# Row sums that divide late: a DRAM detour for the softmax denominators of five head pairs

## The chip, the cores and the metric

One core of a Trainium2 chip runs the whole kernel. The metric is the device time of one execution in microseconds (us); the value of a kernel is the median of its runs. The engines are TensorE (PE, with its weight loads as PEld), VectorE (DVE), ScalarE (ACT), GpSimd (POOL) and SyncE (SP), which here only issues DMA transfers.

## The reference, cut to what matters

A trunk of two layers over 1024 tokens of width 1024 in fp32. Each layer is a token mixer of 12 heads (64 wide) beside a memory attention of 4 heads, then an output projection and a gated MLP with a causal convolution. Layer 0 mixes with causal softmax attention and a forget bias, layer 1 with rotary embedding and a dilated attention. What the change touches is the softmax and what follows it:

```python
sc = jnp.where(kpos[None, :] <= qpos[:, None], sc, NEG)
p = jax.nn.softmax(sc, axis=-1)
return jnp.einsum('bhqk,bhkd->bhqd', p.astype(v.dtype), v)
...
heads = jnp.concatenate([mix, mem_out], axis=1)
h = h + merge_heads(heads) @ w_out[layer]
```

Layer 1's three dilated branches, weighted by their log-sum-exps, come out as one softmax over all keys with a bias table, so both layers run the same block code.

## The kernel before

fp32 products are built from two fp32r halves ("hi" and "lo") with three matmuls per product. Activations lie feature-major: 128 partitions are two heads (a "head pair"), the free dimension is tokens.

A layer has an attention phase and an MLP phase. The attention phase first projects the memory and runs memory attention, then walks 96 blocks: 6 head pairs `p`, two heads `hh` each, 8 query blocks `i` of 128 tokens. For a block, `scores` (line 371) makes the scores on PE; one DVE instruction adds the bias, scales by -1/8 and keeps the row minimum (line 383); ACT takes the exponential into `y` and accumulates the row sum (line 387); DVE takes the reciprocal of the row sum (line 389) and multiplies `y` by it (line 390). Two blocks later `transpose_p` (line 392) transposes `y` on PE through one of two "tp" banks; ACT casts the bank to `pth` (line 397) and DVE subtracts to get `ptl` (line 398). Three blocks after the scores, and for two blocks at once, line 701 multiplies with the values on PE. `fold` (line 400) adds the halves of the result, ACT first (405) and DVE after it (406), and stores the tile in DRAM, `o_scr` (line 412); only for the last pair does it go straight to the output projection's operand.

Between the blocks a filler (`Fill`) puts the projections of the next pair on PE: `proj_q`, `proj_k` (with its moves of K halves between partitions on SP's queue, line 95), `proj_v`, and near the end `out_part`, the output projection over the first seven of eight result tiles. Its operand comes from `load_o` (line 246): it reads seven tiles back from `o_scr` in the order 0, 1, 2, 3, 6, 7, 4 into `oraw` (line 253; tag `sq`, five buffers of 128x512 that the rotary embedding and `fold` use too), ACT casts to the high half (line 254), GpSimd subtracts to the low half (line 255). Tiles 6 and 7 are the memory heads. It runs once per half of the tokens and layer. In layer 1 the rotary embedding of Q and K (lines 328 to 333) adds copies on ACT, a product on GpSimd and a sum on DVE.

PE's order is the program's (`manual_schedule`); the order on the other engines and on SP's queue comes from the framework's scheduler, and each engine then works through its list in order.

Of the kernel before, what the change touches and what calls it, by code (L numbers as in the profile page):

```python
# [6 lines left out]
F32 = mybir.dt.float32  # L7
R32 = mybir.dt.float32r
BF16 = mybir.dt.bfloat16
AF = mybir.ActivationFunctionType  # L10
ALU = mybir.AluOpType
AX = mybir.AxisListType

P = 128
T = 1024
KD = 8
NT = T // P
HT = 512
MT = 256
NMIX = 12  # L20
NPAIR = NMIX // 2
# [8 lines left out]
def trunk(ctx, tc, a, out):  # L30
    nc = tc.nc
    sb = ctx.enter_context(tc.tile_pool(name="sb", bufs=1))
    pp = ctx.enter_context(tc.tile_pool(name="ps", bufs=1, space=bass.MemoryType.PSUM))
    dram = ctx.enter_context(tc.tile_pool(name="dram", bufs=1, space=bass.MemoryType.DRAM))
# [11 lines left out]
    def yt(name):  # L46
        return sb.tile([P, T], F32, tag="P", name=name, bufs=3)

    def tab(name):
        return sb.tile([P, T], F32, tag="tab", name=name, bufs=3)  # L50

    def sqt(name, dt=F32):
        return sb.tile([P, HT], dt, tag="sq", name=name, bufs=5)

    def small(name, w=4, tag="m", bufs=8):
        return sb.tile([P, w], F32, tag=tag, name=name, bufs=bufs)
# [3 lines left out]
    def bank(tag, name="bk"):  # L60
        return pp.tile([P, HT], F32, tag=tag, name=name, bufs=NB[tag])
# [14 lines left out]
    trim = sb.tile([P, P], BF16, name="trim")  # L76
    gains = sb.tile([P, 7, KD], F32, name="gains")
    mhalf = sb.tile([P, 4], F32, name="mhalf")
    zero = sb.tile([P, MT], BF16, name="zero")
    nc.vector.memset(ones, 1.0)  # L80
    nc.vector.memset(mhalf, -0.5)
    nc.vector.memset(zero, 0.0)
    warm = small("warm")
    nc.scalar.activation(warm, mhalf, AF.Square)
    nc.scalar.dma_start(gains, a["gains"])
# [2 lines left out]
    nc.scalar.dma_start(trim, a["c_trim"])  # L88

    o_scr = [[dram.tile([P, T], F32, name=f"oscr{l}_{c}") for c in range(KD)] for l in range(2)]  # L90
    h_scr = [[dram.tile([P, HT], F32, name=f"hscr{c}_{h}") for h in range(2)] for c in range(KD)]
    c_scr = dram.tile([NMIX, T], F32, name="cscr")

# [19 lines left out]
    def x_tiles(half):  # L113
        return (sb.tile([P, KD, HT], R32, tag=f"xh{half}", name=f"xh{half}"),
                sb.tile([P, KD, HT], R32, tag=f"xl{half}", name=f"xl{half}"))
# [130 lines left out]
    def load_o(l, half):  # L246

        if (l, half) in O:
            return O[l, half]
        oh, ol = O[l, half] = x_tiles(half)  # L250
        for c in KORD[:-1]:
            raw = sqt("oraw")
            nc.sync.dma_start(raw, o_scr[l][c][:, half * HT:half * HT + HT])
            nc.scalar.copy(oh[:, c, :], raw)  # L254
            nc.gpsimd.tensor_tensor(ol[:, c, :], raw, oh[:, c, :].bitcast(F32), op=ALU.subtract)  # L255
        return oh, ol
# [21 lines left out]
    def attention_phase(l):  # L278
        with tc.manual_schedule(engines={mybir.EngineType.PE}):
# [88 lines left out]
                return proj_k(3 + 2 * p, half, ops[p], l == 1)  # L368


            def scores(y, m, qst, kst, klt, i, nk, bias, tri):
                qs = slice(i * P, (i + 1) * P)
                npc = (nk + HT - 1) // HT
                for pc in range(npc):
                    c0, c1 = pc * HT, min(nk, pc * HT + HT)
                    s = bank("s")
                    mask = tri and pc == npc - 1
                    sw = s[:, :c1 - c0]
                    nc.tensor.matmul(sw, lhsT=qst[:, qs], rhs=kst[:, c0:c1], start=True, stop=False)
                    nc.tensor.matmul(sw, lhsT=qst[:, qs], rhs=klt[:, c0:c1], start=False, stop=not mask)  # L380
                    if mask:
                        nc.tensor.matmul(s[:, c1 - c0 - P:c1 - c0], lhsT=identb, rhs=trim, start=False, stop=True)
                    nc.vector.tensor_tensor_reduce(  # L383
                        out=y[:, c0:c1], in0=sw, in1=bias(c0, c1), scale=-0.125,
                        scalar=BIG if pc == 0 else m[:, pc - 1:pc],
                        op0=ALU.add, op1=ALU.min, accum_out=m[:, pc:pc + 1])
                nc.scalar.activation(y[:, :nk], y[:, :nk], AF.Exp, bias=m[:, npc - 1:npc], scale=-1.0,  # L387
                                     accum_out=m[:, 2:3])
                nc.vector.reciprocal(m[:, 3:4], m[:, 2:3])
                nc.vector.tensor_scalar(y[:, :nk], y[:, :nk], m[:, 3:4], None, op0=ALU.mult)  # L390

            def transpose_p(y, j0, nj, ph, pl):
                tp = bank("tp").rearrange("p (j q) -> p j q", j=4)
# [6 lines left out]
            def fold(o, odd, c, half):  # L400

                rows = slice(64, 128) if odd else slice(0, 64)
                other = slice(0, 64) if odd else slice(64, 128)
                t = sqt("fold")
                nc.scalar.copy(t[rows, :], o[other, :])
                nc.vector.tensor_tensor(t[rows, :], o[rows, :], t[rows, :], op=ALU.add)
                if c == NPAIR - 1:
                    oh, ol = load_o(l, half)
                    nc.scalar.copy(oh[rows, c, :], t[rows, :])
                    nc.vector.tensor_tensor(ol[rows, c, :], t[rows, :], oh[rows, c, :].bitcast(F32), op=ALU.subtract)  # L410
                    return
                nc.sync.dma_start(o_scr[l][c][rows, half * HT:half * HT + HT], t[rows, :])

            def new_m():
                return small("m")
# [82 lines left out]
            def forget():  # L498

                cu = yt("cu")  # L500
                nc.scalar.dma_start(cu, a["c_cum"])
                w = NT * NMIX
                zf = z.rearrange("p t h -> p (t h)")
                e = [sqt(f"fz{i}")[:, :w] for i in range(4)]
                nc.vector.scalar_tensor_tensor(e[0], zf, -1.0, zf, op0=ALU.mult, op1=ALU.max)
                nc.scalar.activation(e[0], e[0], AF.Exp, scale=-1.0)
                nc.vector.tensor_scalar(e[1], e[0], 1.0, None, op0=ALU.add)
                nc.vector.tensor_scalar(e[2], e[1], -1.0, None, op0=ALU.add)
                nc.vector.tensor_tensor(e[0], e[0], e[2], op=ALU.subtract)
                nc.vector.reciprocal(e[2], e[1])  # L510
                nc.vector.tensor_tensor(e[0], e[0], e[2], op=ALU.mult)
                nc.scalar.activation(e[1], e[1], AF.Ln)
                nc.vector.tensor_tensor(e[0], e[0], e[1], op=ALU.add)
                lf = e[3]
                nc.vector.scalar_tensor_tensor(lf, zf, 0.0, e[0], op0=ALU.min, op1=ALU.subtract)
                yield None
                crow = yt("crow")
                for half in range(2):
                    ps = psp()
                    nt = 4 * half + 4  # L520
                    for t in range(nt):
                        c0 = max(t * P - half * HT, 0)
                        g0 = half * HT + c0 - t * P
                        nc.tensor.matmul(ps[:NMIX, c0:HT], lhsT=lf[:, t * NMIX:(t + 1) * NMIX],
                                         rhs=cu[:, g0:g0 + HT - c0], start=(t == 0), stop=(t == nt - 1))
                    nc.scalar.copy(crow[:NMIX, half * HT:half * HT + HT], ps[:NMIX, :])
                nc.sync.dma_start(c_scr, crow[:NMIX, :])
# [98 lines left out]
            if l == 0:  # L626
                f = forget()
# [32 lines left out]
            st = {}  # L660
            D = 2

            def emit_s(s):
                p, hh, i = seq[s]
                qst, kst, kl = ops[p]["q"], ops[p]["k"], ops[p]["kl"]
                if i == 0 and l == 0:
                    cb = tab("cb")
                    nc.sync.dma_start(cb, c_scr[2 * p + hh:2 * p + hh + 1, :].to_broadcast([P, T]))
                    st["cb"] = cb
                if l == 0:  # L670
                    cb = st["cb"]
                    bias = lambda c0, c1: cb[:, c0:c1]
                else:
                    bias = lambda c0, c1: toep[:, (7 - i) * P + c0:(7 - i) * P + c1]
                y, m = yt("y"), new_m()
                scores(y, m, qst[hh], kst[hh], kl[hh], i, (i + 1) * P, bias, l == 0)
                st["y", s] = y

            def emit_t(s):
# [29 lines left out]
            for s in range(len(seq) + D + 1):  # L709
                if s < len(seq):  # L710
                    p, i = s // 16, s % 16
# [246 lines left out]
```

## Time and profile before

| | |
|---|---|
| median of 3 runs | 2702.18 us (2698.43 to 2704.3) |
| profiled execution | 2700.07 us |
| its span, first to last instruction | 2698.3 us |
| mean granted TensorE clock | 0.983 |
| busy: PE, DVE, ACT, POOL | 2549.5, 1449.2, 1113.6, 889.8 us |

The attention phases lie at about 0 to 600 us and 1350 to 1950 us, the MLP phases after each. In the rows, "L390" is line 390; `out<-in` are the program's tile names; "<-" in brackets names what ended the idle time ahead of an instruction.

### The profile page before, as it was taken

To read this page: it belongs to the slowest core of one execution; us is meant where nothing else is said; L and a number is where in the kernel's file an instruction comes from. 1 tells how busy PE (TensorE), PEld (TensorE's weight loads), DVE (VectorE), ACT (ScalarE), POOL (GpSimd) and SP (SyncE) were. 2 spreads that over 40 slices of the span, in tenths; PEclk is the share of its full clock that TensorE was granted. 3 is DMA by queue.
4 is the path that set the end of the run, shared out by engine and by line. 5 is a ranking of instruction groups with operands and counts; after the bars stand their busy time and mean duration, and the time that the engine had idled before them with its cause. 6 is when DMAs were issued, how large, how long until landed. Compare 5 with 4: busy or idle time off the path is not lost. (4 is left out here: it accounts for less than half of the span.)

```text
span 2698.3 us, 34564 instructions
## 1 busy us (share of the span) xinstructions
PE 2549.5 (94%) x12808; PEld 2125.7 (79%) x12808; DVE 1449.2 (54%) x2879; ACT 1113.6 (41%) x2149; POOL 889.8 (33%) x650
## 2 busy tenths in 40 slices
PE   5899999989999999999998999989899999999997
PEld 4878888767888888888777787867688888888886
DVE  6667777565424343434766767665654343433345
ACT  5555555544313231223356767665433222222222
POOL 4210101454323232323552333335443232233232
PEclk8999999999999999999999999999999999999998
DMA  5121223422111111112431212133211111111112
GB/s 162 55 83 56 74 60 100 143 67 63 54 48 47 47 48 54 48 47 63 132 106 46 55 38 57 38 106 128 74 48 47 50 52 48 47 47 50 52 47 94
DMA packets 98896, 180.95 MB, mean 67 GB/s; under 512 B 12700, under 2 KB 15388, under 8 KB 98728
## 3 DMA queue, kind: packets, MB, share of 16 engines
q1 hardware_dynamic: 97864, 178.06, 21.6%
q8 instruction: 101, 1.65, 0.3%
q10 hardware_dynamic: 864, 0.69, 0.1%
q14 instruction: 67, 0.55, 0.1%
HBM read 148.24 MB, written 15.78 MB: 61 GB/s over the span
## 5 line engine op out<-in xcount | busy, mean ns | idle before, releaser
L110 POOL TENSOR_TENSOR wlo<-wraw,whi 128x512 fp32r<-128x512 f32 x450 | 590.2, 1331 | 1422.3 <-ACT whi L109 1328.3
L162 PE MATMUL bk<-xh,whi 128*128 128x512 f32 x2112 | 857.4, 406 | 34.6 <-ACT xh L254 11.6
L163 PE MATMUL bk<-xl,whi 128*128 128x512 f32 x2112 | 832.4, 394 | 5.8 <-POOL xl L255 3.1
L164 PE MATMUL bk<-xh,wlo 128*128 128x512 f32 x2112 | 831.5, 394 | 1.0 <-POOL wlo L110 1.0
L109 ACT CAST whi<-wraw 128x512 fp32r<-128x512 f32 x450 | 268.6, 616 | 644.9 <-PE bk L163 442.4
L162 PEld LDWEIGHTS bk<-xh,whi 128*128 128x128 f32 x2112 | 402.5, 191 | 116.9 <-ACT xh L254 13.6
L164 PEld LDWEIGHTS bk<-xh,wlo 128*128 128x128 f32 x2112 | 400.7, 190 | 86.8 <-POOL wlo L110 1.7
L163 PEld LDWEIGHTS bk<-xl,whi 128*128 128x128 f32 x2112 | 402.2, 190 | 83.2 <-POOL xl L255 6.4
L162 PE MATMUL bk<-gh,whi 128*128 128x512 f32 x704 | 276.1, 392 | 1.2 <-DVE h L259 1.1
L776 DVE SCALAR_TENSOR_TENSOR gate<-bk,cw,gate 128x511 f32<-128x511 f32 (+1 forms) x176 | 131.3, 746 | 271.5 <-ACT gate L774 270.0
L163 PE MATMUL bk<-gl,whi 128*128 128x512 f32 x704 | 274.6, 390 | 0.0
L164 PE MATMUL bk<-gh,wlo 128*128 128x512 f32 x704 | 274.5, 390 | 0.0
L259 DVE TENSOR_TENSOR h<-h,bk 128x512 f32<-128x512 f32 x208 | 141.7, 685 | 236.3 <-PE bk L164 236.3
L387 ACT ACTIVATE y<-y,m 128x128 f32<-128x128 f32 (+1 forms) x192 | 149.2, 778 | 106.5 <-DVE m L383 104.1
L776 DVE SCALAR_TENSOR_TENSOR val<-bk,cw,val 128x511 f32<-128x511 f32 (+1 forms) x176 | 131.1, 745 | 114.6 <-ACT val L774 113.0
L398 DVE TENSOR_TENSOR ptl<-bk,pth 128x512 fp32r<-128x512 f32 (+3 forms) x288 | 152.8, 551 | 66.1 <-ACT pth L397 65.4
L397 ACT CAST pth<-bk 128x512 fp32r<-128x512 f32 (+3 forms) x288 | 131.0, 479 | 93.1 <-PE bk L396 90.8
L396 PE MATMUL bk<-ident,y 128*128 128x128 f32 x864 | 130.2, 277 | 33.1 <-DVE ptl L398 32.9
L162 PEld LDWEIGHTS bk<-gh,whi 128*128 128x128 f32 x704 | 132.6, 188 | 31.2 <-DVE h L259 2.8
L163 PEld LDWEIGHTS bk<-gl,whi 128*128 128x128 f32 x704 | 132.6, 188 | 27.7 <-issue 0.5
L164 PEld LDWEIGHTS bk<-gh,wlo 128*128 128x128 f32 x704 | 132.4, 188 | 27.6
L792 DVE TENSOR_TENSOR gl<-val,gh 128x1024 fp32r<-128x1024 f32 x44 | 53.9, 1226 | 175.4 <-ACT gh L791 175.4
(160 smaller groups left out, 3585.6 us busy)
## 6 DMA issues: line engine op xcount, KB each, us to landing
wraw<-in_wu SPq DMA_DIRECT2D x176, 256.0 KB, 2.8
wraw<-in_wd SPq DMA_DIRECT2D x104, 256.0 KB, 2.8
wraw<-in_wo SPq DMA_DIRECT2D x64, 256.0 KB, 2.8
wraw<-in_wq SPq DMA_DIRECT2D x56, 256.0 KB, 2.9
oscr<-fold SPq DMA_DIRECT2D x56, 128.0 KB, 2.2
oraw<-oscr SPq DMA_DIRECT2D x28, 256.0 KB, 3.7
cb<-cscr SPq DMA_DIRECT2D x12, 512.0 KB, 3.9
wraw<-in_wv SPq DMA_DIRECT2D x20, 256.0 KB, 2.9
```

The source lines that it names most:

```text
L109: nc.scalar.copy(hi[:, w], raw[:, :n])
L110: nc.gpsimd.tensor_tensor(lo[:, w], raw[:, :n], hi[:, w].bitcast(F32), op=ALU.subtract)
L162: nc.tensor.matmul(ps, lhsT=whi(k), rhs=xhi(k), start=(first and k == 0), stop=False)
L163: nc.tensor.matmul(ps, lhsT=whi(k), rhs=xlo(k), start=False, stop=False)
L164: nc.tensor.matmul(ps, lhsT=wlo(k), rhs=xhi(k), start=False, stop=(last and k == nk - 1))
L259: nc.vector.tensor_tensor(H[half](n), (src or H[half])(n), ps, op=ALU.add)
L387: nc.scalar.activation(y[:, :nk], y[:, :nk], AF.Exp, bias=m[:, npc - 1:npc], scale=-1.0, accum_out=m[:, 2:3])
L396: nc.tensor.transpose(tp[:, jj, :], y[:, j * P:(j + 1) * P], ident)
L397: nc.scalar.copy(ph, tp[:, :nj, :])
L398: nc.vector.tensor_tensor(pl, tp[:, :nj, :], ph.bitcast(F32), op=ALU.subtract)
L776: nc.vector.scalar_tensor_tensor(t[:, o + d:o + HT], ps[:, :HT - d], w(2 - d), t[:, o + d:o + HT], op0=ALU.mult, op1=ALU.add)
L792: nc.vector.tensor_tensor(gl, v, gh.bitcast(F32), op=ALU.subtract)
```

## The change

For the first five head pairs the exponentials stay undivided. The row sums of four blocks gather in one tile of four columns, `den`; after each fourth block DVE takes the reciprocal of all four columns, and a DMA writes them into a row of DRAM, `r_scr`, one row of 1024 tokens per head. The stored result tiles are thus too large by the row sum. When `load_o` reads back a tile of these pairs, it also reads the two reciprocal rows, each broadcast to 64 partitions, and DVE multiplies the tile by them before the cast. The last pair and the memory heads keep dividing their probabilities. An unused tile of zeros and its memset go.

```diff
-    zero = sb.tile([P, MT], BF16, name="zero")
-    nc.vector.memset(zero, 0.0)
...
+    r_scr = [[dram.tile([2, T], F32, name=f"rscr{l}_{c}") for c in range(NPAIR - 1)] for l in range(2)]
...
             raw = sqt("oraw")
-            nc.sync.dma_start(raw, o_scr[l][c][:, half * HT:half * HT + HT])
+            hs = slice(half * HT, half * HT + HT)
+            nc.sync.dma_start(raw, o_scr[l][c][:, hs])
+            if c < NPAIR:
+                rb = sqt("orb")
+                for hh in range(2):
+                    nc.sync.dma_start(rb[64 * hh:64 * hh + 64, :], r_scr[l][c][hh:hh + 1, hs].to_broadcast([64, HT]))
+                nc.vector.tensor_tensor(raw, raw, rb, op=ALU.mult)
             nc.scalar.copy(oh[:, c, :], raw)
...
                 nc.scalar.activation(y[:, :nk], y[:, :nk], AF.Exp, bias=m[:, npc - 1:npc], scale=-1.0,
-                                     accum_out=m[:, 2:3])
-                nc.vector.reciprocal(m[:, 3:4], m[:, 2:3])
-                nc.vector.tensor_scalar(y[:, :nk], y[:, :nk], m[:, 3:4], None, op0=ALU.mult)
+                                     accum_out=m[:, 2:3] if den is None else den)
+                if den is None:
+                    nc.vector.reciprocal(m[:, 3:4], m[:, 2:3])
+                    nc.vector.tensor_scalar(y[:, :nk], y[:, :nk], m[:, 3:4], None, op0=ALU.mult)
...
-                scores(y, m, qst[hh], kst[hh], kl[hh], i, (i + 1) * P, bias, l == 0)
+                if p < NPAIR - 1 and i % 4 == 0:
+                    st["den"] = small("den", 4, "den", 3)
+                den = st["den"] if p < NPAIR - 1 else None
+                scores(y, m, qst[hh], kst[hh], kl[hh], i, (i + 1) * P, bias, l == 0,
+                       None if den is None else den[:, i % 4:i % 4 + 1])
+                if den is not None and i % 4 == 3:
+                    nc.vector.reciprocal(den, den)
+                    with nc.allow_non_contiguous_dma(reason="one value per query"):
+                        nc.sync.dma_start(r_scr[l][p][hh, (i - 3) * P:(i + 1) * P].rearrange("(t q) -> q t", q=P), den)
```

## Rows read from the trace of the kernel before

**Rows 1.** Busy by stretch: us, PE, PEld, DVE, ACT, POOL, PEclk, DMA share, GB/s.

```profile
600.00:1400.00 800.00, 791.17 (x3524) 653.21 (x3523) 359.74 (x546) 245.64 (x383) 292.74 (x206) 1.00 0.21 64
...
165.00:455.00 290.00, 278.86 (x1801) 241.67 (x1800) 210.34 (x566) 162.12 (x372) 35.83 (x28) 0.99 0.25 71
1510.00:1800.00 290.00, 265.45 (x1663) 232.07 (x1663) 198.99 (x534) 194.14 (x418) 99.30 (x77) 0.99 0.18 49
```

**Rows 2.** Waits of PE, 165 to 455 us: total us, times, longest.

```profile
PE bk L396 <- DVE ptl L398: 8.8, 10, 1.8
...
PE bk L701 <- DVE ptl L398: 0.8, 2, 0.5
```

**Rows 3.** Waits of PE, 1510 to 1800 us.

```profile
PE bk L396 <- DVE ptl L398: 17.7, 14, 2.7
PE bk L701 <- DVE ptl L398: 5.2, 10, 1.0
...
PE bk L380 <- DMA kla<-kla: 0.3, 1, 0.3
```

**Rows 4.** Groups by line: busy us, mean ns, idle before them and its releaser.

```profile
L390 DVE TENSOR_SCALAR y<-y,m 128x128 f32<-128x128 f32 (+1 forms) x192 | 115.0, 599 | 5.0
...
L389 DVE RECIPROCAL m<-m 128x1 f32<-128x1 f32 x192 | 31.1, 162 | 88.6 <-ACT y L387 87.9
```

**Rows 5.** Timelines of DVE and ACT near 450 us: start, us, instruction.

```profile
448.50 1.01 DVE L390 TENSOR_SCALAR y<-y,m 128x128 f32<-128x128 f32 x1
...
450.27 1.16 DVE L398 TENSOR_TENSOR ptl<-bk,pth 128x512 fp32r<-128x512 f32 x2
...
449.11 0.97 ACT L397 CAST pth<-bk 128x512 fp32r<-128x512 f32 x2
```

**Rows 6.** Timelines of DVE and ACT near 1599 us.

```profile
1599.79 0.89 DVE L398 TENSOR_TENSOR ptl<-bk,pth 128x512 fp32r<-128x512 f32 x2
...
1598.74 0.75 ACT L397 CAST pth<-bk 128x512 fp32r<-128x512 f32 x2
```

**Rows 7.** Timeline of DVE near 1509 us, layer 1.

```profile
1508.48 0.69 DVE L331 TENSOR_TENSOR ropeq<-bk,ropec 128x512 f32<-128x512 f32 x1 [1.29 <-ACT ropeqs L330]
...
1509.83 1.74 DVE L333 TENSOR_TENSOR ropeq<-ropeq,ropeqs 128x512 f32<-128x512 f32 x1
```

**Rows 8.** Timeline of PE near 1510 us, layer 1.

```profile
1509.84 0.66 PE L396 MATMUL bk<-ident,y 128*128 128x128 f32 x4 [1.12 <-DVE ptl L398]
1512.09 0.65 PE L396 MATMUL bk<-ident,y 128*128 128x128 f32 x4 [1.60 <-DVE ptl L398]
```

**Rows 9.** Busy by stretch, around the wait near 450 us.

```profile
445.00:455.00 10.00, 8.18 (x48) 7.00 (x47) 8.44 (x22) 6.18 (x15) 2.59 (x2) 0.84 0.34 107
```

**Rows 10.** Waits of PE over the whole span, for the cast in `load_o`.

```profile
PE bk L162 <- ACT xh L254: 11.6, 3, 5.2
```

**Rows 11.** Timelines of PE at the two first halves of `load_o`.

```profile
485.76 0.67 PE L162 MATMUL bk<-xh,whi 128*128 128x512 f32 x1 [3.88 <-ACT xh L254]
...
1819.48 0.79 PE L162 MATMUL bk<-xh,whi 128*128 128x512 f32 x1 [5.22 <-ACT xh L254]
...
1824.83 0.79 PE L162 MATMUL bk<-xh,whi 128*128 128x512 f32 x1 [2.53 <-ACT xh L254]
```

**Rows 12.** Timeline of POOL, first half of `load_o`, layer 1.

```profile
1824.86 7.46 POOL L255 TENSOR_TENSOR xl<-oraw,xh 128x512 fp32r<-128x512 f32 x6 [3.83 <-ACT xh L254]
```

**Rows 13.** Busy by stretch, first half of `load_o`, layer 0.

```profile
484.00:494.00 10.00, 7.00 (x18) 4.15 (x18) 1.37 (x5) 4.85 (x10) 6.69 (x6) 0.66 0.87 252
```

**Rows 14.** Group of line 437, DVE.

```profile
L437 DVE TENSOR_TENSOR ym<-ym,mm 128x512 f32<-128x512 f32 x32 | 22.7, 709 | 0.9
```

**Rows 15.** DMA issues: count, KB each, median us to landing.

```profile
oscr<-fold SPq DMA_DIRECT2D x56, 128.0 KB, 2.2
oraw<-oscr SPq DMA_DIRECT2D x28, 256.0 KB, 3.7
...
gains<-in_gains ACTq DMA_DIRECT2D x1, 28.0 KB, 3.8
```

More of the change, by code (lines that the diff above doesn't have):

```diff
@@ L368, in pair_k, with scores @@
                 return proj_k(3 + 2 * p, half, ops[p], l == 1)
-            def scores(y, m, qst, kst, klt, i, nk, bias, tri):
+            def scores(y, m, qst, kst, klt, i, nk, bias, tri, den):
                 qs = slice(i * P, (i + 1) * P)
```

## The prediction

> **What bounds the kernel now.** I read busy time by stage first, then who TensorE (PE) waited for, then the timelines of the places where it waited. In the MLP between 600 and 1400 us PE is busy 791 of 800 us and VectorE (DVE) 360 [rows 1], so nothing that the change does to DVE can count there. The attention phases are where PE has holes. In pairs 0 to 4 of layer 0 (165 to 455 us) it is idle 290.00 - 278.86 = 11.1 us, in those of layer 1 (1510 to 1800 us) 290.00 - 265.45 = 24.6 us [rows 1]. DVE is only 69 to 73% busy there, so it is no bound by its sum; it hurts where it is late. PE's order is written out by hand and the change does not touch it; what counts is only how long PE stands before a given matmul.
>
> PE waits in those stretches almost only for `ptl` (line 398), DVE's subtraction, which frees the PSUM bank that the next transposes want, or makes the low half that the value matmuls read: 8.8 + 0.8 = 9.6 us in layer 0 [rows 2], 17.7 + 5.2 = 22.9 us in layer 1 [rows 3]. That is the whole pool from which a relief of DVE can be paid, 32.5 us. The reader is to see how small it is beside the work removed.
>
> **What goes.** 160 of 192 blocks lose the reciprocal (line 389) and the scaling (line 390). DVE's busy time falls by 160/192 of 31.1 + 115.0 us, 122 us, and the 87.9 us in which it stood before line 389 until ScalarE's (ACT) exponential was through goes in the same share, 73 us [rows 4]. Added on DVE: 40 reciprocals of 4 columns at line 389's 0.16 us (6 us; each still waits for its exponential, but once in four blocks) and 20 products of 128x512. DVE is relieved by some 100 us of work.
>
> How much of it reaches PE is read from what stands ahead of `ptl`. Three kinds of place:
> - DVE itself is the line. Around 450 us a scaling of 1.01 us stands in front, and `ptl` starts at 450.27; ACT's casts for it began at 449.11 and two took 0.97, so the first was done near 449.7 [rows 5]. Without the scaling `ptl` starts some 0.57 us sooner, and then ACT's cast is what is late. PE's wait there is the longest of layer 0, 1.8 us [rows 2]: a third of it goes.
> - The fold. `ptl` starts at 1599.79, with scaling and reciprocal ahead of it on DVE; ACT's two casts ran from 1598.74 for 0.75 [rows 6], the first ready near 1599.33, so 0.46 us goes.
> - Rotary embedding, layer 1 alone. DVE stood 1.29 us until ACT's copies `ropeqs` were through, and its sum `ropeq` then took 1.74 us [rows 7]. Nothing of this is removed. PE waited 1.12 and 1.60 us there [rows 8]; the pair of waits comes three times, and a wait of 2.7 us [rows 3] twice, the same `ropeq` behind it: 13.5 of the 22.9 us. I take nothing off them.
>
> So of 9.6 us and of 22.9 - 13.5 = 9.4 us I take 45%: 8.5 us. DVE's shorter queue also lets the row minima, and so the exponentials that wait for them, start sooner; no row prices that. It is 0 if ACT is late in any case, and at most the rest, 24 us; I take 4, near zero, because in all three kinds ACT comes last. Then the granted clock: the 10 us around the wait near 450 have 0.84 instead of 1.00 [rows 9], 1.6 us of PE work; with that wait cut I take 1.5 back. Relief: 8.5 + 4 + 1.5 = 14 us, bounds 4 and 32.
>
> **What comes.** `load_o` reads back result tiles, four times in all (two halves, two layers). Each time five of seven tiles now take three transfers instead of one, a slot of the `sq` pool (5 buffers) for the row sums, and a product on DVE ahead of ACT's cast. PE waits three times for these casts, 11.6 us in all [rows 10], and the timeline has all three in first halves: 3.88 (layer 0), 5.22 and 2.53 (layer 1) [rows 11]. Second halves are not waited for; their loads lie ahead of the matmuls, and I cost them at 0, with 3 us each if that cover is gone. In the first halves PE stands with nothing else to do, so a longer load goes straight into the span.
>
> Its price per first half, from both sides. Below: 0, if the three transfers overlap and GpSimd's subtraction, 7.46 us for six tiles anyway [rows 12], stays the pace. By bytes: ten transfers of 128 KB more are 1.31 MB; in the heart of the load the queues are 0.87 busy and move 252 GB/s [rows 13], so 5.2 us. By slots: a round of load (3.7 us [rows 15]), product (0.7), cast (0.5, as in [rows 5]) and subtraction (1.24) is 6.1 us, and five slots hold two and a half tiles with their sums, so five such tiles take 12.3 us where subtraction needs 6.2: 6.1 us more. I take 3.5 us, between nothing and the bytes, for the first tile is loaded ahead of the rest and the two unscaled tiles catch up; and 0.5 us because PE runs this stretch at a granted clock of 0.66 [rows 13], between its two levels of 1.2 and 2.4 GHz, and stays there longer. Twice 4 is 8 us; bounds 0 and 14.
>
> The product is taken at 0.71 us from line 437, the same shape from SBUF [rows 14]; from above it is line 333's 1.74 us, two SBUF inputs while GpSimd worked [rows 7]. The Trainium skill, "SBUF — State Buffer", Who interferes with whom, says that a DVE instruction with two SBUF inputs contends with GpSimd's reads of SBUF. The row of 1.74 us agrees; by the rule every product in `load_o` stands beside GpSimd's subtractions, and the slot bound grows by about 1 us a round.
>
> The 40 writes of row sums (128 partitions x 4 values) go out on SyncE's (SP) queue between the K moves (line 95), the stores of `fold` and the weights. A write waits for its reciprocal, and what stands behind it waits too: mostly weight loads, far ahead of PE. Its own duration no row shows: from below 2.2 us (a 128 KB store), from above four times the 3.8 us of a transfer with 128 short rows, since it has 512 pieces, 15 us [rows 15]. I take 4 us, near the store, and at that nothing is late. Memset and `zero` tile: nothing, they lie in the start, ahead of the first loads' landing.
>
> **Sum.** -14 + 8 = -6 us. The profiled execution took 2700.07 us; 2700.07 - 6 = 2694, and as it lies 2.1 us below the median of the runs, 2696 is the forecast. 0.2% is 5.4 us, about what a measurement of this kernel can tell from no change.
>
> **Rivals.**
> - *The load becomes the longer wait (slower).* If slots set the pace, each first half costs 6.1 us and, for products held up by GpSimd, 1 us in each of two rounds; second halves lose their cover, 3 us each: 2 x (8.1 + 3) = 22 us against 14: +8, 2710. For it: the queues are nearly full there already, and PE stands idle. Against it: first halves alone were waited for. It decides from a load stretch that is 7 us longer than before in each layer.
> - *The small writes hold up the K moves (slower).* In layer 1 PE already waited 0.3 us for a K move to land [rows 3], so these have no slack. At the bound of 15 us instead of 4 a move right behind a write is 11 us late; at five pairs of layer 1 that is 55 us, and at a third of it, since not every move follows a write closely, 18: -6 + 18 = +12, 2714. The Trainium skill, "DMA: Bandwidth & Descriptors", Rules for kernel authors, says that a transfer with a strided last dimension becomes one descriptor per element; no row of before shows such a transfer.
> - *DVE's relief pays in full (faster).* If the exponentials move up with the minima, most of the 32.5 us goes, less rope waits that ACT and GpSimd make: 24 us, with the load at 6: -18, 2684.
> - *No change to be seen.* If ACT is late everywhere, 4 us of relief meet 4 of load: 2702.
>
> **Chances.** The forecast 0.48 (half of it beyond 0.2%, half within), relief in full 0.20, load 0.16, K moves 0.08, no change 0.08. Faster by over 0.2%: 0.24 + 0.20 = 0.44. Within: 0.24 + 0.08 = 0.32. Slower: 0.24. The range reaches to the rivals on both sides, 2681 to 2714; the forecast's own range is 2688 to 2703.
>
> **What would show it.** DVE's busy time near 1350 us; PE's waits for `ptl` down from 32.5 to about 20 us with the rope ones standing; first-half waits for the cast of `load_o` longer, some 7 us more over both layers; no wait for a K move. Wrong would be: `ptl` waits gone altogether, or as large as before; PE waiting in the second halves of `load_o`; a write of row sums that lands in over 8 us.

## The result: slower, 2724.35 us

The changed kernel took 2724.35 us, the median of four runs (2723.70 to 2725.90), beside 2701.43 for the kernel before, measured with it: a ratio of 1.0085, 95% interval 1.007 to 1.010. It is slower by 23 us, above the top of the predicted range. The profiled execution took 2725.9 us, 2724.1 of it span. VectorE's (DVE's) busy time fell from 1449.2 to 1374.3 us, so the work did go; the time did not follow.

Busy by stretch, changed kernel (us, PE, PEld, DVE, ACT, POOL, granted clock, DMA share, GB/s). The first and third rows answer to [rows 1].

```profile
165.00:455.00 290.00, 285.18 (x1861) 248.83 (x1860) 168.17 (x450) 166.62 (x384) 35.64 (x28) 1.00 0.32 72
455.00:600.00 145.00, 119.37 (x574) 93.43 (x574) 84.99 (x177) 65.09 (x132) 54.39 (x41) 0.88 0.41 121
1510.00:1800.00 290.00, 265.74 (x1668) 232.35 (x1669) 160.65 (x413) 194.05 (x421) 100.78 (x77) 0.99 0.22 51
1800.00:1950.00 150.00, 117.86 (x562) 92.86 (x562) 85.77 (x180) 70.55 (x143) 62.59 (x47) 0.87 0.39 116
```

The same view of the kernel before, for the two stretches that were not shown:

```profile
455.00:600.00 145.00, 128.27 (x662) 102.79 (x662) 90.06 (x202) 75.59 (x153) 60.11 (x46) 0.95 0.34 105
1800.00:1950.00 150.00, 129.19 (x637) 103.98 (x636) 85.80 (x179) 75.12 (x149) 76.42 (x58) 0.94 0.36 114
```

In the pairs of layer 0 DVE sheds 42 us and TensorE (PE) gains 6.3 of its 11.1 idle us. In the pairs of layer 1 DVE sheds 38 us and PE gains 0.3. In the two stretches where results are read back, PE is busy 9 and 11 us less than before, at a lower granted clock. These stretches are fixed in time, and work that comes later falls out of them; the comparison matmul by matmul, below, is the safer one.

PE's waits over the whole span (total us, times, longest):

```profile
PE bk L402 <- DVE ptl L404: 28.0, 22, 2.7
PE bk L161 <- ACT xh L259: 26.5, 6, 12.6
PE bk L161 <- ACT xh L415: 12.5, 2, 6.5
...
PE bk L384 <- DMA ka<-ka: 0.6, 2, 0.4
...
PE bk L385 <- DMA kla<-kla: 0.3, 1, 0.3
```

Line 259 is the cast of `load_o`: 11.6 us in three waits [rows 10] have become 26.5 in six. Line 415 is the cast of pair 5's own fold, which ends a second half. For K moves PE waits 0.9 us in all, where it was 0.3 [rows 3].

PE's timeline at the places of [rows 11], then at the two second halves:

```profile
481.72 0.79 PE L161 MATMUL bk<-xh,whi 128*128 128x512 f32 x1 [8.60 <-ACT xh L259]
...
498.82 0.50 PE L161 MATMUL bk<-xh,whi 128*128 128x512 f32 x1 [1.59 <-ACT xh L259]
...
1833.51 0.80 PE L161 MATMUL bk<-xh,whi 128*128 128x512 f32 x1 [12.64 <-ACT xh L259]
...
564.24 0.79 PE L161 MATMUL bk<-xh,whi 128*128 128x512 f32 x1 [6.00 <-ACT xh L415]
...
1915.49 0.80 PE L161 MATMUL bk<-xh,whi 128*128 128x512 f32 x1 [6.50 <-ACT xh L415]
```

PE's order is the same in both kernels (12808 matmuls), so the start of the n-th in one trace can be set beside that of the n-th in the other; the times below are those of the kernel before. At 455 us the changed kernel is 9.0 us ahead. The first half of layer 0 turns that into 5.3 us behind at 540 us (14.3 us lost), its second half into 7.6 at 600 us (2.3 more). The pairs of layer 1 win back 1.1 by 1800 us. Its first half costs 14.3 by 1880 us, its second 4.7 by 1950; the end is 25.8 us behind. In sum some 10 us gained, 28.6 lost in first halves, 7.0 in second halves. One and the same kernel traced twice (e10 and e18 below) differs from itself by up to 3.4 us in this way, so the first halves stand clear of that, and a second half by itself hardly.

The two first halves, matmul for matmul: layer 0, then layer 1, first the kernel before,

```profile
455.00:540.00 85.00, 78.14 (x429) 63.73 (x429) 51.16 (x133) 46.45 (x100) 30.27 (x23) 0.96 0.43 132
...
1800.00:1880.00 80.00, 68.22 (x353) 55.97 (x352) 44.71 (x109) 45.22 (x95) 40.42 (x32) 0.91 0.48 148
```

then the changed one:

```profile
446.00:545.30 99.30, 83.69 (x430) 66.66 (x429) 55.33 (x131) 44.27 (x96) 28.41 (x22) 0.88 0.45 127
...
1806.50:1900.90 94.40, 73.48 (x353) 58.68 (x352) 51.12 (x113) 42.95 (x91) 38.73 (x30) 0.84 0.47 137
```

PE stands 8.8 us longer in the one and 9.1 in the other. The rest, 5.6 and 5.3 us, is the same matmuls taking longer, at a granted clock of 0.88 and 0.84 where it was 0.96 and 0.91.

The two waits at second halves were shorter in the kernel before:

```profile
556.59 0.49 PE L162 MATMUL bk<-xh,whi 128*128 128x512 f32 x1 [3.69 <-ACT xh L409]
...
1890.48 0.49 PE L162 MATMUL bk<-xh,whi 128*128 128x512 f32 x1 [2.56 <-ACT xh L409]
```

What is late there now is on DVE's timeline of the changed kernel:

```profile
558.41 0.69 DVE L258 TENSOR_TENSOR oraw<-oraw,orb 128x512 f32<-128x512 f32 x1 [2.38 <-POOL wlo L109]
559.02 0.68 DVE L388 CUSTOM_DVE_ANT_0 y<-bk,cb 128x512 f32<-128x512 f32 x1
...
1909.67 0.69 DVE L258 TENSOR_TENSOR oraw<-oraw,orb 128x512 f32<-128x512 f32 x1 [2.89 <-DMA orb<-rscr]
1910.28 0.68 DVE L388 CUSTOM_DVE_ANT_0 y<-bk,toep 128x512 f32<-128x512 f32 x1
```

PE has made the last block's scores by 555.2 and 1905.8 us, but their row minimum (line 388) stands in DVE's order behind the product of the last tile read back, and DVE is idle 2.38 and 2.89 us until that tile's row is there. It lands at 558.29 and 1909.55 us. GpSimd's `wlo`, which the first line names, ended in the same instant, but the product reads nothing of it. The exponential, the fold and the fold's cast all follow the minimum.

How a first half goes now is seen on SyncE's (SP's) queue in layer 0, where PE arrives at 473 us:

```profile
472.81 0.58 SPq L253 DMA_DIRECT2D oraw<-oscr  x1
473.48 0.46 SPq L94 DMA_DIRECT2D kb<-kb  x1
474.64 0.46 SPq L418 DMA_DIRECT2D oscr<-fold  x1
475.16 0.59 SPq L94 DMA_DIRECT2D klb<-klb  x1
476.00 1.11 SPq L257 DMA_DIRECT2D orb<-rscr  x2
```

and on DVE:

```profile
480.33 0.69 DVE L258 TENSOR_TENSOR oraw<-oraw,orb 128x512 f32<-128x512 f32 x1 [3.22 <-DMA orb<-rscr]
482.15 1.42 DVE L258 TENSOR_TENSOR oraw<-oraw,orb 128x512 f32<-128x512 f32 x1 [1.13 <-DMA orb<-rscr]
...
496.81 0.69 DVE L388 CUSTOM_DVE_ANT_0 y<-bk,cb 128x512 f32<-128x512 f32 x1 [6.13 <-PE bk L385]
...
497.42 0.69 DVE L258 TENSOR_TENSOR oraw<-oraw,orb 128x512 f32<-128x512 f32 x1
```

The raw tile is asked for at 472.81, its row only at 476.00, behind two K moves and a fold's store. Product, cast and PE follow at 480.33, 481.05 and 481.72. The last tile shows a second thing: its product is queued on DVE behind a row minimum that itself waits for PE's scores, and PE then stands 1.59 us for the cast behind that product.

DMA issues of the changed kernel (count, KB each, median us to landing), which answer to [rows 15], and one wait on SP's queue:

```profile
oscr<-fold SPq DMA_DIRECT2D x56, 128.0 KB, 2.2
...
orb<-rscr SPq DMA_DIRECT2D x40, 128.0 KB, 4.0
...
rscr<-den SPq DMA_DIRECT2D x40, 2.0 KB, 8.4
```

```profile
SPq L253 <- POOL xl L260: 16.2, 12, 2.3
```

The loads of raw tiles waited 16.2 us, twelve times, for GpSimd (POOL) to give back a slot of the `sq` pool; in the kernel before it was 10.3 us, seven times.

### The profile page after: what moved, and what is told of

Same layout as the page of the kernel before. It is cut to its first block, busy times and chain, and to the rows that moved or that the text cites. A ratio compares the mean times of both kernels' runs of the same rounds, so it can differ in the third digit from the quotient of the medians.

```text
span 2724.1 us, 34573 instructions
## 1 busy us (share of the span) xinstructions
PE 2558.5 (94%) x12808; PEld 2132.2 (78%) x12808; DVE 1374.3 (50%) x2618; ACT 1111.9 (41%) x2149; POOL 892.5 (33%) x650
## 5 line engine op out<-in xcount | busy, mean ns | idle before, releaser
L161 PE MATMUL bk<-xh,whi 128*128 128x512 f32 x2112 | 859.1, 407 | 55.8 <-ACT xh L259 26.5
```

The source lines that it names most:

```text
L161: nc.tensor.matmul(ps, lhsT=whi(k), rhs=xhi(k), start=(first and k == 0), stop=False)
```

## Experiments

Each median stands beside that of the kernel before measured with it; line numbers in the rows are each kernel's own.

| run | us | before | ratio, 95% interval |
|---|---|---|---|
| e1_relief | 2688.54 | 2701.74 | 0.9951, 0.9937 to 0.9966 |
| e2_load | 2741.66 | 2701.74 | 1.0152, 1.0137 to 1.0167 |
| e3_nowrite | 2732.90 | 2701.74 | 1.0115, 1.0098 to 1.0131 |
| e4_slots | 2710.95 | 2701.74 | 1.0037, 1.0023 to 1.0050 |
| e5_const | 2701.68 | 2700.04 | 1.0007, 0.9997 to 1.0016 |
| e6_first | 2708.69 | 2700.04 | 1.0032, 1.0020 to 1.0044 |
| e7_fold | 2724.72 | 2700.04 | 1.0092, 1.0075 to 1.0109 |
| e8_folddve | 2717.21 | 2700.04 | 1.0062, 1.0047 to 1.0077 |
| e9_early | 2709.49 | 2699.90 | 1.0038, 1.0023 to 1.0053 |
| e10_bearly | 2685.04 | 2699.90 | 0.9949, 0.9932 to 0.9965 |
| e11_four | 2695.49 | 2699.90 | 0.9979, 0.9969 to 0.9988 |
| e12_layer0 | 2691.20 | 2699.90 | 0.9966, 0.9954 to 0.9978 |
| e13_poolearly | 2718.97 | 2702.32 | 1.0063, 1.0048 to 1.0078 |
| e14_poollayer0 | 2695.51 | 2702.32 | 0.9974, 0.9963 to 0.9986 |
| e15_constpool | 2710.55 | 2702.32 | 1.0036, 1.0023 to 1.0049 |
| e16_pool | 2725.40 | 2702.32 | 1.0091, 1.0076 to 1.0106 |
| e17_four0 | 2682.51 | 2699.00 | 0.9937, 0.9924 to 0.9951 |
| e18_bearly5 | 2684.99 | 2699.00 | 0.9948, 0.9935 to 0.9960 |

### The change taken apart: e1, e2, e3, e5

The relief alone, e1_relief (from the changed kernel):

```
-            if c < NPAIR:
-                rb = sqt("orb")
-                ... (row loads, product)
-                    nc.sync.dma_start(r_scr[l][p]..., den)
```

> The probabilities of pairs 0 to 4 stay undivided and the reciprocals of the row sums are still taken, but the sums are not written, not read back and not multiplied: this leaves out the division of those five pairs. It is the relief alone. Theory A (all that was lost was lost where the halves are read back): about 2691 us, which is the time of before less the 9.7 us by which the changed kernel's matmuls ran ahead up to the read-backs. The prediction's term of 14 us would give 2687 us; 2701 us or more would mean that the relief bought nothing.

It gained 13.2 us. Busy by stretch, pairs of layer 0 and of layer 1:

```profile
165.00:455.00 290.00, 285.18 (x1858) 248.71 (x1857) 167.65 (x447) 165.89 (x383) 35.67 (x28) 1.00 0.24 72
1510.00:1800.00 290.00, 266.41 (x1682) 232.80 (x1682) 163.51 (x424) 197.19 (x426) 99.32 (x76) 0.99 0.21 58
```

PE gains 6.3 us in the pairs of layer 0 and 1.0 in those of layer 1, against [rows 1]. Matmul by matmul, 9.6 of the 10.6 us by which this trace ends ahead come between 165 and 455 us. So the relief is real, and is nearly all layer 0's.

The read-back alone, e2_load (from the kernel before; `r_scr` here is one row of ones stored at the start):

```
             nc.sync.dma_start(raw, o_scr[l][c][:, hs])
+            if c < NPAIR:
+                rb = sqt("orb")
+                for hh in range(2):
+                    nc.sync.dma_start(rb[64 * hh:64 * hh + 64, :], r_scr[l][c]...)
+                nc.vector.tensor_tensor(raw, raw, rb, op=ALU.mult)
```

> The kernel before with divided probabilities, and beside them the read-back of the changed kernel: ten loads of a row per half and the five products, of rows of ones that were written once at the start. It is the price of the read-back alone. Theory A: about +33 us, 2735 us, since the matmuls of the changed kernel fell back by 27 us in the two first halves and by 8 us in the two second halves. Rival B (the read-back is cheap, and the small writes and the row sums are what delays it): under +10 us, 2712 us at most.

It cost 39.9 us. Of these, 6.6 were there before 78 us, where the store of the ones stands among the first loads, so the read-back costs 33, as theory A had it. By trace the two first halves cost 13.5 and 13.8 us, the second halves 2.3 and 3.9, much as in the changed kernel.

Without the small writes, e3_nowrite (`r_one` as in e2):

```
-                        nc.sync.dma_start(r_scr[l][p]..., den)
+    r_scr = [[r_one] * (NPAIR - 1)] * 2
```

> The changed kernel without its 40 writes of four columns of reciprocals; the loads of the read-back fetch rows of ones, so the division of the five pairs is left out. Rival B (the writes, 8.4 us each from issue to landing, hold the queue and the loads behind them): over 5 us faster than the changed kernel, below 2719 us. Theory A: within 2 us of its 2724 us, since the writes of the pairs lie tens of microseconds ahead of the loads.

It was 8.5 us slower than the changed kernel, which neither theory expected. Matmul by matmul it was 6.7 us behind it by 63 us of the span, again at the store of the ones, and 6.3 at the end: nothing for all that follows. Forty writes less bought nothing, so they are not the cause.

The product alone, e5_const:

```
-                rb = sqt("orb")
-                ... (row loads)
-                nc.vector.tensor_tensor(raw, raw, rb, op=ALU.mult)
+                nc.vector.tensor_tensor(raw, raw, oneb, op=ALU.mult)
...
-                        nc.sync.dma_start(r_scr[l][p]..., den)
```

> Neither the small writes nor the row loads; the five raw tiles of each half are multiplied by a tile of ones that lies in SBUF. This leaves out the division of the five pairs and is the price of the products alone. Theory P (the product costs what it takes in each tile's chain, 0.7 to 1.6 us, and is hidden behind the raw loads of the next tiles): 2 to 6 us above the relief alone, 2690 to 2695 us. Rival (the products, slowed beside GpSimd's subtractions, set the pace of the first halves): more than 12 us above it, over 2700 us.

Twenty products, and nothing to load for them, take back the whole relief: 2701.68 us, 1.6 above before where e1 was 13.2 below. Theory P falls, and the time is its rival's. PE's waits:

```profile
PE bk L162 <- ACT xh L257: 13.2, 4, 6.9
...
PE bk L162 <- ACT xh L413: 7.6, 2, 3.8
```

In e1 these were 11.9 and 4.5 us. No single wait explains the cost; those for the casts, a fold, GpSimd's subtractions and `ptl` grew by 1 to 3 us each. Matmul by matmul against e1, some 5 us of the cost lie in the first halves and some 8 in the second.

### Slots and the order of the queue: e4, e6

e4_slots (the rows in the 4 KB slots of the projections):

```
-                rb = sqt("orb")
+                if c % 2 == 0:
+                    rbt = qk("orb", F32)
+                rb = rbt[:, (c % 2) * HT:(c % 2) * HT + HT]
```

> The changed kernel with the five row tiles of each half in the three slots of 4 KB that the query and key projections use (two rows in one), in place of the slots of 2 KB which they share with the raw tiles and the fold copies. Theory S (the read-back waits for slots, so that its loads are issued late): the first halves lose less, 6 to 14 us off 2724 us. Theory L (what counts is the load of 4 us and the product in each tile's own chain): within 3 us of 2724 us.

13.4 us came back, in the upper half of what theory S expected. Matmul by matmul most of it is layer 1's, whose first half costs 5.0 us instead of 14.3; that of layer 0 still costs 11.6. With the raw tiles alone in `sq`, their loads wait for POOL as in the kernel before:

```profile
SPq L253 <- POOL xl L262: 10.3, 7, 2.6
```

and PE, in the first half of layer 0, waits once and then has its tiles:

```profile
486.51 0.79 PE L161 MATMUL bk<-xh,whi 128*128 128x512 f32 x1 [13.84 <-ACT xh L261]
```

That one wait is longer than the 8.60 above. SP's queue shows what it is for: the rows went out early, the raw tile after the K moves:

```profile
466.94 4.35 SPq L259 DMA_DIRECT2D orb<-rscr  x7
476.05 0.48 SPq L94 DMA_DIRECT2D ka<-ka  x1
479.06 0.48 SPq L94 DMA_DIRECT2D kla<-kla  x1
479.59 0.58 SPq L253 DMA_DIRECT2D oraw<-oscr  x1
```

e6_first (all row loads of a half written ahead of its raw loads, same slots):

```
+        for c in range(NPAIR - 1):
+            ... rbs[c] = a half of a projection slot; two row loads
         for c in KORD[:-1]:
             raw = sqt("oraw")
```

> The changed kernel with all ten row loads of a half issued ahead of its raw loads, and the rows in the projections' slots. Theory Q (what is left of the loss in the run with other slots is the place of the raw loads in SyncE's queue, behind ten row loads and the K moves): no better than that run, 2708 to 2716 us. If the late landing of the rows set the wait, it would be better by 3 us or more, below 2708 us.

2708.69 us, level with e4, as theory Q had it: it is not the rows' landing that is left.

### The products moved to the folds: e7, e8

```
-            if c < NPAIR:
-                ... (row loads and product in load_o)
...
+                rb = sqt("orb")
+                nc.sync.dma_start(rb[rows, :], r_scr[l][c][int(odd):int(odd) + 1, hs]...)
+                def finish():                      # called two blocks later
+                    nc.gpsimd.tensor_tensor(t[rows, :], t[rows, :], rb[rows, :], op=ALU.mult)
+                    nc.sync.dma_start(o_scr[l][c][rows, hs], t[rows, :])
```

> The reciprocals are loaded as rows where the fold of each head and half is made, two blocks later GpSimd multiplies the 64x512 fold tile by them and it is stored divided; the halves are read back as in the kernel before. Theory A (the relief of 13 us holds, and the loss is that of the place of the loads and products in the read-back): 2689 to 2697 us, faster than before. Rival (the row load waits some 8 us for its small write at the head of SyncE's queue and holds up the K moves behind it, or the fold tiles hold slots which the projections need): 2702 us or more.

> As the run with the products at the folds, with VectorE in place of GpSimd. Forty 64x512 products of about 0.7 us put 28 us back on VectorE, where the division of the blocks took about 75 us. Theory A: 2690 to 2700 us, up to 5 us above the run with GpSimd; rival (a product that waits for its row holds up the subtractions behind it in VectorE's order): above 2705 us.

Both missed: +24.7 and +17.2 us. In the run with GpSimd PE waits

```profile
PE bk L161 <- ACT xh L254: 27.6, 2, 14.3
...
PE bk L379 <- DMA ka<-ka: 8.1, 4, 4.4
```

The wait for K moves is the rival's; the read-back is still late although it loads no rows (14.3 us, 5.2 before); why is open. With VectorE the K moves were not waited for, but the value matmuls' wait for `ptl` was 14.0 us, where the relief alone has 5.5.

### Reading back earlier: e9 to e12

e9_early is e4 with one step moved, e10_bearly the kernel before with the same:

```
                     if i in (0, 4):
                         fill.need(("ab"[i // 4], p))
+                    if s == 80:
+                        load_o(l, 0)
```

> The run with the rows in the projections' slots, and the first half of each layer is read back at block 80, ahead of the last K projection and its moves, in place of block 83. Theory W (TensorE's waits of 13.8 and 10.5 us at the two first halves come from loads issued late, behind the K moves): they shrink below 4 us each, 12 to 18 us off that run's 2711 us, 2693 to 2699 us. Rival (casts and products only come as fast as before, and the last K projection is held up by them): 2707 us or more.

> The kernel before with that one step alone: the first halves are read back at block 80. Its three waits for the cast of the read-back (11.6 us) should go: 2690 to 2694 us. It is the control for the run with the change: if both gain the same, the early read-back is no merit of the undivided probabilities.

The control gained 14.9 us and the change nothing: 2685.04 against 2709.49, which was 2710.95 in e4. In e10 PE no longer waits for the cast of `load_o` at all, and it keeps its clock in both stretches:

```profile
455.00:600.00 145.00, 131.83 (x697) 107.59 (x697) 95.73 (x208) 76.60 (x156) 65.83 (x49) 0.98 0.34 110
1800.00:1950.00 150.00, 135.47 (x676) 109.73 (x675) 93.68 (x181) 76.90 (x151) 80.60 (x60) 0.99 0.33 112
```

In e9 that wait has gone too, but another came in its place. PE's waits, and DVE's timeline:

```profile
PE bk L717 <- DVE ptl L406: 30.3, 22, 11.0
```

```profile
468.33 0.69 DVE L260 TENSOR_TENSOR oraw<-oraw,orb 128x512 f32<-128x512 f32 x1 [5.36 <-DMA orb<-rscr]
468.94 0.68 DVE L406 TENSOR_TENSOR ptl<-bk,pth 128x512 fp32r<-128x512 f32 x1
...
483.68 0.69 DVE L260 TENSOR_TENSOR oraw<-oraw,orb 128x512 f32<-128x512 f32 x1 [8.71 <-DMA orb<-rscr]
```

DVE stands 5.36 and 8.71 us in front of products whose rows have not landed, with the subtractions that PE needs behind them. PE also waits 5.2 us once for a K move, as the rival had it, and the time is the rival's.

e11_four leaves pair 4 divided as well, e12_layer0 all of layer 1 (both from e9):

```
-            if c < NPAIR:            -                if p < NPAIR - 1 and i % 4 == 0:
+            if c < NPAIR - 2:        +                if p < NPAIR - 2 and i % 4 == 0:      (e11)
+            if c < NPAIR and l == 0: +                if p < NPAIR - 1 and l == 0 and ...   (e12)
```

> As the run with the early read-back, with four of six pairs undivided: pair 4, whose tile is the last of each half to be read back, keeps its division. A fifth of the relief goes (2.6 us of 13), and the product that lies last in each second half goes with it. If the products in the second halves cost what the run with the constant tile showed (about 8 us of its 13 in the two layers), this is 2 to 6 us faster than the five pairs with the early read-back; if not, 2 to 3 us slower.

> As the run with the early read-back, with undivided probabilities in the first layer only. In the trace of the relief alone the matmuls gain some 10 us in the first layer and under 3 us in the second. If the second layer's read-back still costs more than its relief, this is 3 to 8 us faster than the run with both layers; if the early read-back hides it, it is up to 3 us slower.

Fewer undivided pairs, less time: 14.0 us less than e9 without pair 4, where 2 to 6 were expected, and 18.3 without layer 1, where 3 to 8 were. Why it is so much more is not shown. Both are faster than the kernel before, and both slower than e10, which has none.

### Which engine multiplies: e13 to e16

One edit in four kernels (e9, e12, e5 and the changed kernel):

```
-                nc.vector.tensor_tensor(raw, raw, ...)
+                nc.gpsimd.tensor_tensor(raw, raw, ...)
```

> The run with the constant tile of ones, with its products on GpSimd; the division of the five pairs is left out. Theory D (most of the product's 13 us is what it takes from VectorE, by its order and by being drawn out beside GpSimd): 2689 to 2696 us. Rival L (it is the length of the chain load, product, cast): GpSimd's product is no shorter, so 2701 us or more.

> The changed kernel with the products on GpSimd and nothing else. Theory D: 8 to 14 us off 2724 us, 2710 to 2716 us. Rival L, or a bound by the slots and SyncE's queue whoever multiplies: 2720 us or more.

> The run with the early read-back of both layers, with the ten products of each layer on GpSimd. Theory D (in that run a product which waits for its row stands in VectorE's order ahead of the subtractions of the transposes, and TensorE's waits of 4.6, 7.3 and 11.0 us for them are its cost): those waits go, 15 to 22 us off 2709 us, 2687 to 2695 us. Rival (GpSimd's own subtractions and the K moves behind the loads on SyncE's queue come late instead): 2703 us or more.

> The run with undivided probabilities in the first layer only and the early read-back, with the products on GpSimd. Theory D: TensorE's two waits of 4.6 and 7.4 us for the subtractions go: 2677 to 2684 us, level with or under the kernel before with the early read-back alone (2685 us). Rival: 2690 us or more, no better than with VectorE.

Theory D fell in all four: 8.2 us above before in e15 (e5: 1.6), no difference in e16, 7.1 us worse than e9 in e13 and 1.9 worse than e12 in e14, each against the kernel before measured with it. Taking the products off VectorE gains nothing. As one takes 1.14 to 1.34 us on GpSimd (e15), among GpSimd's own subtractions, this does not show that they cost nothing in VectorE's order. In e13 the long waits of the value matmuls went, as expected, but the transposes now waited up to 6.9 us for `ptl`. ACT's timeline shows its place:

```profile
468.77 0.62 ACT L261 CAST xh<-oraw 128x512 fp32r<-128x512 f32 x1 [4.78 <-POOL oraw L260]
...
472.66 0.62 ACT L261 CAST xh<-oraw 128x512 fp32r<-128x512 f32 x1 [2.88 <-POOL oraw L260]
473.18 0.96 ACT L405 CAST pth<-bk 128x512 fp32r<-128x512 f32 x2
```

The engine that stands still is now ScalarE: its cast waits for the product, and the casts of the transposes stand behind it.

### What can be kept: e17, e18

e17_four0 joins e11 and e12 (pairs 0 to 3, layer 0 alone, early read-back); e18_bearly5 is e10 again beside it.

```
-            if c < NPAIR and l == 0:
+            if c < NPAIR - 2 and l == 0:
-                if p < NPAIR - 1 and l == 0 and i % 4 == 0:
+                if p < NPAIR - 2 and l == 0 and i % 4 == 0:
```

> Undivided probabilities of pairs 0 to 3 in the first layer only, rows in the projections' slots, products on VectorE, the first halves read back at block 80. If the relief of the first layer (9 us, four fifths of it 7 us) can be kept by leaving out what costs the most (the second layer's read-back, and the product of the tile that is read last), this comes to 2676 to 2682 us, under the kernel before with the early read-back alone (2685 us). If four row loads and products in a half still eat it up, 2685 us or more.

> The kernel before with the early read-back alone, on the same chip and with five rounds, to set the run with four pairs beside it: 2683 to 2688 us.

2682.51 us, just above the range for a relief that is kept, and 2684.99 us. Both beat both kernels, by 14 to 16.5 us over before, and their intervals overlap (0.9924 to 0.9951 and 0.9935 to 0.9960): whether the last 2.5 us are the undivided probabilities' is not settled.

## Why the prediction was wrong

Each run's difference to the kernel before measured with it gives the sum of the change: the relief -13.2 (e1), the products +14.8 (e5 stands at +1.6), the rows with their loads and the writes +7.6 (e4 at +9.2), and rows in the slots of the raw tiles +13.7 (the changed kernel at +22.9). The parts are in this order; in another they need not be the same.

- **The relief was right as a size, in part by luck:** 14 us forecast, 13.2 measured. The place near 450 us did what was forecast: 2.4 us came there between 448 and 455 us, where 0.57 and 1.5 were priced. Another subtraction of DVE stands between the scaling and `ptl` there (`qb` at 449.55 us), and near 1599 us the fold's (1599.06), which the prediction passed over. It was also right that the rotary waits of layer 1 stand: `ptl` there is 18.2 + 3.9 us in the changed kernel, 22.9 before [rows 3]. What was off is where it came from. In the two stretches of pairs the waits for `ptl` are 4.4 + 0.3 and 18.2 + 3.9, 26.8 us, where about 20 of 32.5 were forecast, and nearly all of the relief is layer 0's. There e1 needs 9.6 us less for the same matmuls; 3.3 of these are the clock (PE busy 275.58 us instead of 278.86), where 1.5 was taken in all. DVE's busy time fell to 1374.3 us, where near 1350 was forecast.
- **The step that failed is the price of a first half:** "I take 3.5 us, between nothing and the bytes, for the first tile is loaded ahead of the rest and the two unscaled tiles catch up", 4 us with the clock. Measured: 14.3 us in each, 5.6 and 5.3 of them the clock's, for which 0.5 was taken. The bound by slots had the right mechanism and gave 6.1 us. It left out that a raw tile and its row are two places in SP's queue with K moves and a store between them, 3.2 us apart in the first half of layer 0, and that the chain's late operations stand in the orders of DVE and ACT among those that PE waits for next. e4 prices the slots; the second halves, e9 and e13 show the orders.
- **Second halves at nothing failed too:** they cost 2.3 and 4.7 us, and PE waiting there was named as a sign of being wrong. It is not the cast of `load_o` that PE waits for, as the prediction's 3 us had it, but the cast of pair 5's own fold: 6.00 and 6.50 us, where 3.69 and 2.56 were there before and were passed over. The last product, whose row is late, stands ahead of the last row minimum on DVE.
- **The product's own duration was right as a median** (0.71 us taken; median 0.713), not as a mean (0.957, up to 1.80), and as a price misleading: DVE is busy 1374.3 us with them and 1353.3 without (e1), 19.1 us of that in the products, all in the two stretches where PE stands; and taking them off DVE gave nothing back (e15, e16). The Trainium skill, "SBUF — State Buffer", Who interferes with whom, by which a VectorE instruction with two SBUF inputs contends with GpSimd's reads of SBUF, agrees with the four of 1.42 us and up, each beside one of GpSimd's subtractions. Not every product stood beside one, as the prediction took it: eight of the twenty ran beside none and took 0.68 to 0.69 us, and one, at 1836.29 us, took 0.69 although it ran beside one.
- **The writes** took 8.4 us to land, twice the value taken and over the 8 us named as a sign of being wrong, yet they delayed nothing (e3); that rival is out.
- **The rival that came true** is the load as the longer wait, at +22.9 us instead of +8: its condition (a load stretch 7 us longer in each layer) was met twice over, and the two second halves were in its sum. Its chance of 0.16 was too small, because I priced the first halves near the middle of bounds although [rows 11] show PE standing there with nothing else to do.

Not settled is how the 14.8 us of the products divide between the longer chain and the operations queued behind it, and why the read-back of e7 and e8 is late without any rows.

## What to carry to other kernels

Work taken from an engine that is not the bound pays only the waits that it caused, here 13 us for the 96 us by which DVE's busy time fell in e1 (1449.2 to 1353.3). Work put into a stretch where the bound engine already stands can cost most of what it takes, and far more when its data come late: the twenty products, 21.4 us of DVE's time in e5, cost 14.8 us there with nothing to load, and with their rows, slots and writes 36.1. Before moving work there, look whether that stretch can start earlier: one call moved in the kernel before was worth 15 us, as much as the relief in full. And an operation whose data are late blocked whatever stood behind it on its engine, on VectorE (the second halves, e9) and on ScalarE (e13) alike.

## What the runs showed of the hardware

- A write of 2 KB in 512 pieces took 8.4 us from issue to landing, nearly four times the 2.2 us of a 128 KB store; reading one 2 KB row into 64 partitions (128 KB) took 4.0 us.
- The same 128x512 product took 0.68 to 1.80 us on DVE; on GpSimd, in e15, 1.14 to 1.34 us.
- The granted clock followed PE's stops. In the stretch from 1800 to 1950 us it was 0.99 in e10, where the waits for the read-back are gone, 0.94 in the kernel before and 0.87 in the changed one, each a mean over its two levels of 1.2 and 2.4 GHz. A wait of PE thus costs more than its own length: in the first half of layer 0 PE stood 8.8 us longer than before, and the same matmuls took 83.69 us instead of 78.14.
